# The ends of v's and z's tiles issued in steps behind the next tiles' products, and the up product's output in four DRAM buffers

## The chip, the cores and the metric

The kernel runs on one core of one Trainium2 chip. The metric is the device time of one execution in microseconds (us). Before the change the median of three runs is 2250.19 us (2246.54 to 2250.68). The engines of the core work beside each other, each through its own list of instructions in order: TensorE (PE) does the matrix products, VectorE (DVE), ScalarE (ACT) and GpSimd (POOL) the elementwise work, and SyncE (SP) issues most of the transfers.

## The reference

One layer of a hybrid encoder: a gated MLP branch with a spatial mixer (u, v), a state-space branch (z, xBC, dt), gates, and a feed-forward part. 1024 prompt rows and 64 sample rows share the weights; the model width is 1024, everything is float32. Cut to what matters here:

```python
h = rms_norm(x, pre_mix_w)
u, v, z, xbc, dt_raw, g_a, g_b = jnp.split(h @ w_in, [p1, p2, p3, p4, p5, p6], axis=-1)
u = jax.nn.gelu(u)
v = layer_norm(jax.nn.gelu(v), gmlp_ln_w, gmlp_ln_b)
...
g = y * jax.nn.silu(z)          # gated group RMSNorm of the state-space branch
...
f = jnp.square(jax.nn.relu(rms_norm(x, pre_ffn_w) @ w_up)) @ w_down
x = x + rms_norm(f, post_ffn_w)
```

v has 1024 columns and z has 2048. The hidden width of the feed-forward part is 4096.

## The kernel before

**Stages.** The kernel goes through the first half of z's columns, then v together with z's second half, then the state-space stage, u with the spatial mixer, the two branch products, the output product, the up product and the down product. A float32 product is made of three matmuls on split operands: each operand is a high part (`split`, ACT, line 87) and a low part that is left over (line 88, DVE or POOL).

**z's first half** (lines 442 to 507). `z_tile` multiplies nine row tiles (eight of 128 prompt rows and the sample's) and ends each with a tanh on ACT (L453), a combine on DVE (L454) and a store from POOL's queue (L455).

**v and z's second half** (lines 506 to 582, called here the product stage). Each is a block of 1024 columns; v is `b = 0`, z's part `b = 1`. Rows and columns are halved, and a Strassen-like plan of seven products, `P2, P1, P6, P5, P7, P3, P4`, makes the four quarters. A product has four tiles of 128 rows by 512 columns (`m` = 0 to 3), each of 12 matmuls (lines 517 to 519), and the 64 sample rows go along in separate small products (`sample`). Chained products add into the four PSUM banks `X`: P1, P6, P7 and P4 go into the same bank of a tile one after the other, and the bank is read in between. P2, P5 and P3 use other banks, `ps`. What follows each tile:

- P2: ACT copies `ps` out (`cz`, L551). P6 and P5: ACT copies too (L557, L560), and after P5 DVE adds (L561).
- P1, P7, P3: DVE adds (L553, L563, L566), then the tile is finished with `epi`. P4's tiles are finished from PSUM directly.
- `epi` (lines 313 to 332) for v is a gelu with LayerNorm sums: square on ACT (L319), scale on POOL (L320), product on DVE (L321), tanh on ACT (L322), combine on DVE (L324), store from POOL's queue (L325), then three ACT instructions that form the sums (L330 to L332). For z it is a silu: tanh on ACT (L317), combine on DVE, store.
- `sample_out` (line 346) first folds the sample's two halves of partitions together with a transfer from SBUF to SBUF (`su`, L354) and an addition (L355), then calls `epi`.

After each tile, work for later products is slipped in: for even `m` a weight piece of the next product is split (`prep`), for odd `m` a piece of the product after that is loaded and, on POOL, added up (`build`, lines 389 to 404).

**Buffers.** The tiles `cz`, `c1`, `c5`, `sbs`, `sc` and `su` share eight buffers (tag `s2`), the working tiles `t` and `jk` of `epi` three (tag `tm`).

**Order.** The program is written once, and a scheduler that keeps a timeline decides in which order each engine gets its instructions; the engines then work through them in that order. An instruction whose input isn't there holds up what is behind it on its engine.

**Up and down products.** `up` writes its output in the combinations that the down product's seven products read (`C` and `E`, lines 1311 to 1316) into the DRAM tensors `rc_d` and `rs_d` (lines 1317 to 1321), 16 slices `p` one after the other. The down product takes four slices at a time (`b` = 0 to 3): `load_x` reads `rc_d` (L1373), `xs_load` reads `rs_d` (L1480), `load_w` the weights (L1379), and POOL sums weight pieces (L1384). `bcast` spreads `post_ffn_w` over the partitions (L191) for the last step.

Of the kernel before, what the change touches and what calls it, by code (L numbers as in the profile page):

```python
# [15 lines left out]
P = 128  # L16
# [17 lines left out]
TQ = 272  # L34
# [12 lines left out]
def program(tc, a):  # L47
# [3 lines left out]
    with ctx:  # L51
# [17 lines left out]
        rc_d = dram.tile([7, 16, P, 2, TQ], F32, name="rc_d")  # L69
        rs_d = dram.tile([16, P, 2, 64], F32, name="rs_d")  # L70
# [241 lines left out]

        def epi(pool, gelu, c, R, dst, inplace, st=None):

            t = pool.tile([P, 512], F32, tag="tm", bufs=tm_bufs[0], name="t")
            if not gelu:
                s.activation(t[:R], c[:R], AF.Tanh, scale=0.5)  # L317
            else:
                s.activation(t[:R], c[:R], AF.Square)  # L319
                g.tensor_scalar(out=t[:R], in0=t[:R], scalar1=GC * GA3, scalar2=GC, op0=ALU.mult, op1=ALU.add)  # L320
                v.tensor_tensor(out=t[:R], in0=c[:R], in1=t[:R], op=ALU.mult)  # L321
                s.activation(t[:R], t[:R], AF.Tanh)  # L322
            o = c if inplace else t
            v.scalar_tensor_tensor(out=o[:R], in0=t[:R], scalar=1.0, in1=c[:R], op0=ALU.add, op1=ALU.mult)  # L324
            g.dma_start(out=dst, in_=o[:R])  # L325
            if gelu:
                i, l = st
                jk = pool.tile([P, 512], F32, tag="tm", bufs=tm_bufs[0], name="jk")
                sm, nm = vsm[:R, l, i:i + 1], vnm[:R, l, i:i + 1]
                s.activation(jk[:R], o[:R], AF.Copy, accum_out=sm)  # L330
                s.activation(nm, sm, AF.Copy, scale=-1.0 / 512)
                s.activation(jk[:R], o[:R], AF.Square, bias=nm, accum_out=vm2[:R, l, i:i + 1])  # L332
# [14 lines left out]
        def sample_out(pool, gelu, ps, add, dst, st=None):  # L347

            c = pool.tile([P, 512], F32, tag="s2", bufs=s2_bufs[0], name="sc")
            u = pool.tile([P, 512], F32, tag="s2", bufs=s2_bufs[0], name="su")  # L350
            s.activation(c, ps, AF.Copy)
            if add is not None:
                v.tensor_tensor(out=c, in0=add, in1=c, op=ALU.add)
            nc.sync.dma_start(out=u[:64], in_=c[64:128, :])  # L354
            v.tensor_tensor(out=c[:64], in0=c[:64], in1=u[:64], op=ALU.add)  # L355
            epi(pool, gelu, c, 64, dst, True, st)
# [58 lines left out]
        with tc.tile_pool(name="p0", bufs=1, side="right") as p0:  # L415
# [26 lines left out]
            def z_tile(ws, gi, i):  # L442
                R = ROWS[i]
                dst = z_d[i * P:i * P + R, gi * 512:(gi + 1) * 512]
                if i == 8:
                    ps = mm.tile([P, 512], F32, tag="mm", name="ps")
                    sample(ps, 0, lambda q: ws[q], True, False)
                    sample(ps, 1, lambda q: ws[2 + q], False, True)
                    sample_out(p0, False, ps, None, dst)
                    return  # L450
# [36 lines left out]
            for i in range(NT):  # L487
                z_tile(ws, 0, i)
                first(i + 3)
                first_T(i + 2)  # L490
# [3 lines left out]
            for k, i in enumerate((4, 5, 6, 7, 8, 0, 1, 2, 3)):  # L494
                z_tile(ws, 1, i)
                if k in (0, 2, 4, 6):
                    sums_a(k // 2)
# [6 lines left out]
            prep(0, 1)  # L504

        with tc.tile_pool(name="pm", bufs=1, side="right") as pm, tc.tile_pool(name="xp1", bufs=3, space=PSUM) as xp:
            pmx.append(pm)
            s2_bufs[0], tm_bufs[0] = 8, 3
# [20 lines left out]
            for k, (b, n) in enumerate(plan):  # L529
# [12 lines left out]
                for m in range(4):  # L542
                    ps = X[m] if chained else mm.tile([P, 512], F32, tag="mm", name="ps")
                    mms(ps, XN[n], k, m, n == "P1" or not chained, chained)
                    if m % 2 == 0:
                        prep(k + 1, m // 2)
                    else:
                        build(k + 2, m // 2)
                    if n == "P2":
                        cz[m] = s2("cz")  # L550
                        s.activation(cz[m], ps, AF.Copy)  # L551
                    elif n == "P1":
                        v.tensor_tensor(out=cz[m], in0=ps, in1=cz[m], op=ALU.add)  # L553
                        epi(pm, gelu, cz[m], P, out_rows(b, m, 0), True, (m, 0))
# [7 lines left out]
                    elif n == "P7":  # L562
                        v.tensor_tensor(out=c5[m], in0=ps, in1=c5[m], op=ALU.add)  # L563
                        epi(pm, gelu, c5[m], P, out_rows(b, 4 + m, 1), True, (4 + m, 1))
                    elif n == "P3":
                        v.tensor_tensor(out=c1[m], in0=ps, in1=c1[m], op=ALU.add)  # L566
                        epi(pm, gelu, c1[m], P, out_rows(b, m, 1), True, (m, 1))
                    else:
                        epi(pm, gelu, ps, P, out_rows(b, 4 + m, 0), False, (4 + m, 0))
                if n == "P1":  # L570
                    sample(sa, 0, w, True, False)
                    sample_out(pm, gelu, sa, sbs, out_rows(b, 8, 0), (8, 0))
                elif n == "P5":
                    sample(sa, 0, w, False, False)
                elif n == "P3":
                    sample(sa, 1, w, False, True)
                    sample_out(pm, gelu, sa, None, out_rows(b, 8, 1), (8, 1))
                if n == "P1" and b == 1:
                    v_stats()
                if n == "P7" and b == 1:  # L580
                    for d, x in b12_parts():
                        nc.sync.dma_start(out=x, in_=d)
        ectx.close()
# [646 lines left out]
        def up_pass(p, tt, prev):  # L1230
# [83 lines left out]
            def post2():  # L1314
                v.tensor_tensor(out=E[:, 1], in0=C[:, 3], in1=E[:, 0], op=ALU.subtract)
                v.tensor_tensor(out=E[:, 3], in0=C[:, 1], in1=E[:, 1], op=ALU.subtract)
                nc.sync.dma_start(out=rc_d[0:2, p, :, tt].rearrange("o p c -> p o c"), in_=C[:, 0:2])
                nc.sync.dma_start(out=rc_d[2, p, :, tt], in_=C[:, 3])
                nc.sync.dma_start(out=rc_d[3:7, p, :, tt].rearrange("o p c -> p o c"), in_=E)
                for hh in range(2):  # L1320
                    nc.sync.dma_start(out=rs_d[p][:, :, hh * 32 + tt * 16:hh * 32 + tt * 16 + 16], in_=C[:, 2 * hh:2 * hh + 2, 256:TQ])
# [25 lines left out]
        bcast(pf, a["post_ffn_w"][0])  # L1347
# [17 lines left out]
        def xload(n, b):  # L1365
            res = []
            for q in range(2):
# [3 lines left out]
                src = rc_d[n, b * 4 + q * 2:b * 4 + q * 2 + 2]  # L1371
# [103 lines left out]
        def xs_load(b):  # L1475
# [3 lines left out]
            for j in range(2):  # L1479
                nc.sync.dma_start(out=raw[:, j], in_=rs_d[b * 4:b * 4 + 4][:, :, j, :].rearrange("q p c -> p q c"))  # L1480
# [15 lines left out]
        xsr = xs_load(0)  # L1496
        load_w(0, "w11")
        load_x(1)
# [4 lines left out]
        for k, (b, n) in enumerate(plan):  # L1503
            last = b == 3
            sl = slots[b]
            if n == "P2":
# [103 lines left out]
```

## Time and profile before

| | us |
|---|---|
| median of three runs | 2250.19 |
| the profiled execution | 2253.99 |
| its span | 2252.3 |
| TensorE busy | 2164.1 (96%) |
| VectorE busy | 1405.2 (62%) |
| ScalarE busy | 966.9 (43%) |
| GpSimd busy | 905.1 (40%) |

Times in the trace count from the start of the span. z's first half takes about the first 140 us, the product stage runs from there to about 310 us, the state-space stage follows; up runs from about 1540 to 1910 us, and down to the end. In the views a row names an engine, the tile written, an arrow and the tile read, and the line (L321 is line 321 of the kernel); a bracket with an arrow gives how long the engine had been idle before and what ended it. "PEclk" is the granted clock of TensorE as a share of full speed.

### The profile page before, as it was taken

What the parts mean: (1) busy time and instruction counts of PE and PEld (TensorE: products, weight loads), DVE (VectorE), ACT (ScalarE), POOL (GpSimd) and SP (SyncE); (2) the same over time, 40 slices, a digit from 0 to 9 for tenths busy, and PEclk for the clock granted to TensorE, in tenths of its full rate; (3) what the DMA queues carried; (4) which work ended last, traced back from release to release, by engine and by line L of the source; (5) the groups of instructions that cost most, each with busy time, mean ns of one, the idle gap of its engine ahead of it and who ended that gap; (6) DMA issues with size and microseconds to landing.
All of it is one profiled execution on the core that took longest, in us unless ns stands there. A gap on an engine that the chain in (4) does not pass through costs nothing.

```text
span 2252.3 us, 33407 instructions
## 1 busy us (share of the span) xinstructions
PE 2164.1 (96%) x12547; PEld 1951.4 (87%) x12547; DVE 1405.2 (62%) x1934; ACT 966.9 (43%) x1911; POOL 905.1 (40%) x888
## 2 busy tenths in 40 slices
PE   8998899999989999999999999998999998999997
PEld 6777689879979879889999999777999998888885
DVE  5846557677677767646632247377555556677777
ACT  5335636355445455433321123245555554433333
POOL 2644421472562652754512545353222223132134
PEclk9999899999999999999999999999999999999999
DMA  6255462253342351542353445443555447534543
GB/s 221 71 182 181 128 203 56 80 138 83 96 129 76 104 143 46 142 134 76 97 170 120 146 118 169 138 164 101 161 153 152 135 154 253 164 106 142 173 122 112
DMA packets 327994, 300.50 MB, mean 133 GB/s; under 512 B 40906, under 2 KB 286364, under 8 KB 327320
## 3 DMA queue, kind: packets, MB, share of 16 engines
q1 hardware_dynamic: 295720, 260.12, 38.8%
q10 hardware_dynamic: 27152, 22.29, 3.0%
q0 software_dynamic: 4960, 15.95, 2.0%
q8 instruction: 99, 1.62, 0.3%
q14 instruction: 63, 0.52, 0.1%
HBM read 220.49 MB, written 77.03 MB: 132 GB/s over the span
## 4 chain that ended last, share of the span: by engine, by line
PE 72%; DVE 7%; DMA 6%; POOL 6%; issue 5%; ACT 3%; SPq 0%; ACTq 0%; POOLq 0%; DVEq 0%
PE ps L125 8%; PE ps L127 8%; PE ps L126 8%; PE X L1241 3%; PE X L1240 3%; PE X L1242 3%; PE X L1391 2%; PE X L1392 2%; PE X L1390 2%; PE ps L978 2%; PE ps L979 2%; PE ps L980 2%; PE ps L1390 2%; DMA bc<-ac_d 2%; PE ps L1392 2%
## 5 line engine op out<-in xcount | busy, mean ns | idle before, releaser
L127 PE MATMUL ps<-hTh,wl 128*128 128x384 f32 (+1 forms) x1152 | 386.5, 336 | 0.0
L125 PE MATMUL ps<-hTh,wh 128*128 128x384 f32 (+1 forms) x1152 | 384.2, 334 | 0.0
L126 PE MATMUL ps<-hTl,wh 128*128 128x384 f32 (+1 forms) x1152 | 384.1, 333 | 0.0
L88 POOL TENSOR_TENSOR wl<-raw,wh 128x1024 fp32r<-128x1024 f32 x74 | 181.8, 2458 | 251.4 <-ACT wh L87 251.4
L127 PEld LDWEIGHTS ps<-hTh,wl 128*128 128x128 f32 x1152 | 217.0, 188 | 9.6 <-issue 9.1
L126 PEld LDWEIGHTS ps<-hTl,wh 128*128 128x128 f32 x1152 | 217.2, 189 | 7.2 <-issue 7.1
L125 PEld LDWEIGHTS ps<-hTh,wh 128*128 128x128 f32 x1152 | 217.1, 188 | 6.6 <-issue 5.6
L87 ACT ACTIVATE wh<-raw 128x1024 fp32r<-128x1024 f32 (+1 forms) x113 | 118.6, 1051 | 239.9 <-PE ps L126 92.7
L643 DVE SCALAR_TENSOR_TENSOR acc<-raw,cw,acc 128x384 f32<-128x384 f32 (+1 forms) x216 | 135.4, 627 | 31.5 <-ACT acc L641 25.4
L1240 PE MATMUL X<-hb,wu 128*128 128x272 f32 x512 | 147.5, 290 | 1.3 <-ACT ev L1247 1.0
L1241 PE MATMUL X<-hb,wu 128*128 128x272 f32 x512 | 147.9, 290 | 0.0
L1242 PE MATMUL X<-hb,wu 128*128 128x272 f32 x512 | 146.1, 290 | 0.0
L1384 POOL TENSOR_TENSOR wd<-wd,wd 128x1024 f32<-128x1024 f32 x32 | 86.0, 2690 | 112.3 <-DVE dl L88 73.2
L762 ACT ACTIVATE bc<-bc,pcum 128x128 f32<-128x128 f32 (+1 forms) x288 | 90.4, 384 | 83.0 <-POOL bc L759 82.8
L979 PE MATMUL ps<-ob,wh 128*128 128x384 f32 (+1 forms) x384 | 125.4, 327 | 0.0
L978 PE MATMUL ps<-ob,wh 128*128 128x384 f32 (+1 forms) x384 | 125.4, 326 | 0.0
L980 PE MATMUL ps<-ob,wl 128*128 128x384 f32 (+1 forms) x384 | 125.3, 326 | 0.0
L87 ACT ACTIVATE dh<-wd 128x1024 fp32r<-128x1024 f32 x56 | 59.0, 1054 | 148.9 <-PE ps L1391 89.8
L88 DVE TENSOR_TENSOR dl<-wd,dh 128x1024 fp32r<-128x1024 f32 x56 | 71.3, 1278 | 47.5 <-ACT dh L87 45.7
L1391 PE MATMUL X<-dl,dh 128*128 128x512 f32 x256 | 99.2, 390 | 0.0
L1392 PE MATMUL X<-dh,dl 128*128 128x512 f32 x256 | 98.9, 389 | 0.0
L88 DVE TENSOR_TENSOR dl<-xd,dh 128x1024 fp32r<-128x1024 f32 x56 | 98.0, 1775 | 1.5 <-PE X L1242 1.2
(459 smaller groups left out, 6022.2 us busy)
## 6 DMA issues: line engine op xcount, KB each, us to landing
raw<-w_in SPq DMA_DIRECT2D x56, 512.0 KB, 4.0
xd<-rc_d SPq DMA_DIRECT2D x112, 256.0 KB, 4.0
rc_d<-E SPq DMA_DIRECT2D x32, 544.0 KB, 3.0
bc<-ac_d SPq DMA_DIRECT2D x64, 256.0 KB, 4.3
raw<-w_branch_b SPq DMA_DIRECT2D x32, 512.0 KB, 3.8
wr<-w_up SPq DMA_DIRECT2D x32, 512.0 KB, 4.0
wd<-w_down SPq DMA_DIRECT2D x16, 1024.0 KB, 5.7
w<-w_in SPq DMA_DIRECT2D x28, 512.0 KB, 3.7
```

Of the source, the lines that this page charges most:

```text
L87: s.activation(hi, src, AF.Copy)
L88: (lo_eng or v).tensor_tensor(out=lo, in0=src, in1=hi, op=ALU.subtract)
L125: pe.matmul(ps[:, :n], wh[:, k, :], hh[:, k, :n], start=(k == 0), stop=False)
L126: pe.matmul(ps[:, :n], wh[:, k, :], hl[:, k, :n], start=False, stop=False)
L127: pe.matmul(ps[:, :n], wl[:, k, :], hh[:, k, :n], start=False, stop=(k == 7))
L978: pe.matmul(ps[:, :n], wh[:, k, :], ob[:, kk, :], start=(k == 0), stop=False)
L979: pe.matmul(ps[:, :n], wh[:, k, :], ob[:, 4 + kk, :], start=False, stop=False)
L980: pe.matmul(ps[:, :n], wl[:, k, :], ob[:, kk, :], start=False, stop=(k == 7))
L1240: pe.matmul(ps, wh[:, k, :], bh[:, k, :], start=start and k == 0, stop=False, skip_group_check=chain)
L1241: pe.matmul(ps, wh[:, k, :], bl[:, k, :], start=False, stop=False, skip_group_check=chain)
L1242: pe.matmul(ps, wl[:, k, :], bh[:, k, :], start=False, stop=k == 3, skip_group_check=chain)
L1392: pe.matmul(ps, xl, wh, start=False, stop=q == 3, skip_group_check=chain)
```

## The change

`epi` and `sample_out` become generators. `end(x)` runs the first step of a tile's end at once and keeps the rest in the list `ends`; `advance(old)` runs one more step of every end that was in the list before the present tile. A gelu end has three steps: square and scale; product and tanh; combine, store and sums. A silu end has two, and the sample's end has one more ahead, up to the `su` transfer. After each tile of the product stage the older ends move one step on, after the new tile's own eviction; at the end of a stage the list is emptied. In z's halves ahead of it only the sample's end is taken in steps. The `tm` tag gets a fourth buffer, and where the result is written in place the sums reuse `t` for their unused output.

`rc_d` and `rs_d` become four tensors each, one for each group of four slices. In the down product the second operand load is written ahead of one weight load, and the broadcast of `post_ffn_w` is written at the third group in place of the beginning.

```diff
-        rc_d = dram.tile([7, 16, P, 2, TQ], F32, name="rc_d")
-        rs_d = dram.tile([16, P, 2, 64], F32, name="rs_d")
+        rc_d = [dram.tile([7, 4, P, 2, TQ], F32, name=f"rc{b}_d") for b in range(4)]
+        rs_d = [dram.tile([4, P, 2, 64], F32, name=f"rs{b}_d") for b in range(4)]
...
+        ends = []
+
+        def end(x):
+            next(x, None)
+            ends.append(x)
+
+        def advance(xs):
+            for x in xs:
+                if next(x, True):
+                    ends.remove(x)
+
         def epi(pool, gelu, c, R, dst, inplace, st=None):
...
                 s.activation(t[:R], c[:R], AF.Square)
                 g.tensor_scalar(out=t[:R], in0=t[:R], scalar1=GC * GA3, scalar2=GC, op0=ALU.mult, op1=ALU.add)
+                yield
                 v.tensor_tensor(out=t[:R], in0=c[:R], in1=t[:R], op=ALU.mult)
                 s.activation(t[:R], t[:R], AF.Tanh)
+            yield
             o = c if inplace else t
...
-                jk = pool.tile([P, 512], F32, tag="tm", bufs=tm_bufs[0], name="jk")
+                jk = t if inplace else pool.tile([P, 512], F32, tag="tm", bufs=tm_bufs[0], name="jk")
...
             nc.sync.dma_start(out=u[:64], in_=c[64:128, :])
+            yield
             v.tensor_tensor(out=c[:64], in0=c[:64], in1=u[:64], op=ALU.add)
-            epi(pool, gelu, c, 64, dst, True, st)
+            yield from epi(pool, gelu, c, 64, dst, True, st)
...
-            s2_bufs[0], tm_bufs[0] = 8, 3
+            s2_bufs[0], tm_bufs[0] = 8, 4
...
+                    old = list(ends)
                     if n == "P2":
                         cz[m] = s2("cz")
                         s.activation(cz[m], ps, AF.Copy)
                     elif n == "P1":
                         v.tensor_tensor(out=cz[m], in0=ps, in1=cz[m], op=ALU.add)
-                        epi(pm, gelu, cz[m], P, out_rows(b, m, 0), True, (m, 0))
+                        end(epi(pm, gelu, cz[m], P, out_rows(b, m, 0), True, (m, 0)))
...
+                    advance(old)
...
+            while ends:
+                advance(list(ends))
...
-        bcast(pf, a["post_ffn_w"][0])
...
-                src = rc_d[n, b * 4 + q * 2:b * 4 + q * 2 + 2]
+                src = rc_d[b][n, q * 2:q * 2 + 2]
...
         xsr = xs_load(0)
+        load_x(1)
         load_w(0, "w11")
-        load_x(1)
...
+            if b == 2 and n == "P2":
+                bcast(pf, a["post_ffn_w"][0])
```

**What moves.** ACT at the turn from v to z, before the change. L551 is z's first eviction, L319 with `X` the square of a tile of v's P4, L330 and L332 the sums of tiles of v's P3 (`c`):

```order
L319 ACTIVATE t<-c_1311 128x512
L331 ACTIVATE vnm<-vsm 128x1
L551 ACTIVATE cz<-ps 128x512
L332 ACTIVATE jk,vm_95<-c_1292,vnm 128x512
L87 ACTIVATE wh<-v_1790 128x1024
L551 ACTIVATE cz<-ps 128x512
L87 ACTIVATE wh<-v_1832 128x1024
L322 ACTIVATE t<-t 128x512
L330 ACTIVATE jk,vsm<-c_1311 128x512
L319 ACTIVATE t<-sc 64x512
```

The same place after the change (L332 is now the square, L336 the tanh, L345 to L347 the sums, L574 z's first eviction):

```order
L345 ACTIVATE t,vsm<-c_1312 128x512
L88 ACTIVATE wh<-w_1654 128x1024
L332 ACTIVATE t<-X 128x512
L346 ACTIVATE vnm<-vsm 128x1
L336 ACTIVATE t<-t 128x512
L88 ACTIVATE wh<-w_1712 128x1024
L347 ACTIVATE t,vm_101<-c_1312,vnm 128x512
L559 ACTIVATE sbs<-sb__1725 128x512
L336 ACTIVATE t<-t 64x512
L332 ACTIVATE t<-X 128x512
L574 ACTIVATE cz<-ps 128x512
```

The squares of two of v's P4 tiles, which stood behind z's evictions, now stand ahead of the first of them, and the sums of v's last P3 tile are done before it.

DVE at the same turn, after the change. L335 is the product, L339 the combine, L89 the low part of a weight piece (`w` for z's P2 and `v` for a later one), L576 the addition after z's P1; the combine that reads `X` is the last to read that bank:

```order
L335 TENSOR_TENSOR t<-X,t 128x512
L89 TENSOR_TENSOR wl<-w_1654,wh 128x1024
L339 SCALAR_TENSOR_TENSOR t<-t,X 128x512
L335 TENSOR_TENSOR t<-sc,t 64x512
L89 TENSOR_TENSOR wl<-w_1712,wh 128x1024
L339 SCALAR_TENSOR_TENSOR sc<-t,sc 64x512
L335 TENSOR_TENSOR t<-X,t 128x512 x2
L339 SCALAR_TENSOR_TENSOR t<-t,X 128x512 x2
L89 TENSOR_TENSOR wl<-v_1776,wh 128x1024
L576 TENSOR_TENSOR cz<-X,cz 128x512
```

Before the change every combine that read `X` stood behind the second weight piece `v` and the first addition of z's P1; now three stand ahead of that.

DVE near the first tiles of v's P5, after the change. L371 folds the sample's halves with `su`, L584 is the addition after P5:

```order
L371 TENSOR_TENSOR sc<-sc,su 64x512
L339 SCALAR_TENSOR_TENSOR cz<-t,cz 128x512
L335 TENSOR_TENSOR t<-sc,t 64x512
L89 TENSOR_TENSOR wl<-v_1258,wh 128x1024
L339 SCALAR_TENSOR_TENSOR sc<-t,sc 64x512
L584 TENSOR_TENSOR c_1233<-ps,c_1233 128x512
```

Before, the fold was followed by a product and a combine of one tile of P1 and by two such pieces, and then came the addition. Now a combine of P1, one piece and the sample's own product and combine stand between them.

On SP, around the last slices of up and the first loads of down, the rows after the change name other tensors and stand in the order they had before: `xd` from `rc_d` (L1398, L1373 before), the weights (L1404), and the broadcast (L192).

```order
L1344 DMA rc_d<-C 128x272
L1347 DMA rs_d<-C 256x1x16
L1343 DMA rc_d<-C 128x2x272
L1347 DMA rs_d<-C 256x1x16
L1345 DMA rc_d<-E 128x4x272
L1398 DMA xd<-rc_d 128x2x256 x2
L192 DMA fin_18236<-post_ffn_w 128x1024
L1441 DMA fin_18237<-x_d 128x1024 x2
```

More of the change, by code (lines that the diff above doesn't have):

```diff
@@ L448, in z_tile @@
                     sample(ps, 1, lambda q: ws[2 + q], False, True)
-                    sample_out(p0, False, ps, None, dst)
+                    end(sample_out(p0, False, ps, None, dst))
                     return
@@ L494, in program @@
             for k, i in enumerate((4, 5, 6, 7, 8, 0, 1, 2, 3)):
+                old = list(ends)
                 z_tile(ws, 1, i)
+                advance(old)
                 if k in (0, 2, 4, 6):
@@ L548, in program @@
                         build(k + 2, m // 2)
+                    old = list(ends)
                     if n == "P2":
@@ L563, in program @@
                         v.tensor_tensor(out=c5[m], in0=ps, in1=c5[m], op=ALU.add)
-                        epi(pm, gelu, c5[m], P, out_rows(b, 4 + m, 1), True, (4 + m, 1))
+                        end(epi(pm, gelu, c5[m], P, out_rows(b, 4 + m, 1), True, (4 + m, 1)))
                     elif n == "P3":
                         v.tensor_tensor(out=c1[m], in0=ps, in1=c1[m], op=ALU.add)
-                        epi(pm, gelu, c1[m], P, out_rows(b, m, 1), True, (m, 1))
+                        end(epi(pm, gelu, c1[m], P, out_rows(b, m, 1), True, (m, 1)))
                     else:
-                        epi(pm, gelu, ps, P, out_rows(b, 4 + m, 0), False, (4 + m, 0))
+                        end(epi(pm, gelu, ps, P, out_rows(b, 4 + m, 0), False, (4 + m, 0)))
+                    advance(old)
                 if n == "P1":
                     sample(sa, 0, w, True, False)
-                    sample_out(pm, gelu, sa, sbs, out_rows(b, 8, 0), (8, 0))
+                    end(sample_out(pm, gelu, sa, sbs, out_rows(b, 8, 0), (8, 0)))
                 elif n == "P5":
@@ L576, in program @@
                     sample(sa, 1, w, False, True)
-                    sample_out(pm, gelu, sa, None, out_rows(b, 8, 1), (8, 1))
+                    end(sample_out(pm, gelu, sa, None, out_rows(b, 8, 1), (8, 1)))
                 if n == "P1" and b == 1:
@@ L582, in program @@
                         nc.sync.dma_start(out=x, in_=d)
+            while ends:
+                advance(list(ends))
         ectx.close()
@@ L1479, in xs_load @@
             for j in range(2):
-                nc.sync.dma_start(out=raw[:, j], in_=rs_d[b * 4:b * 4 + 4][:, :, j, :].rearrange("q p c -> p q c"))
+                nc.sync.dma_start(out=raw[:, j], in_=rs_d[b][:, :, j, :].rearrange("q p c -> p q c"))
             return raw
```

8 lines of the change are left out of this document (4 added, 4 removed).

## The prediction

> **What bounds the kernel now.** I read the page first: TensorE (PE) is busy nearly all the time, so a change of the other engines is worth only what TensorE waits for them.
>
> ```profile
> span 2252.3 us, 33407 instructions
> PE 2164.1 (96%) x12547; PEld 1951.4 (87%) x12547; DVE 1405.2 (62%) x1934; ACT 966.9 (43%) x1911; POOL 905.1 (40%) x888
> ```
>
> 2252.3 - 2164.1 leaves 88 us of TensorE's idle time in the whole span, and the view of what TensorE waited for says where (us in total, times, longest):
>
> ```profile
> PE X L517 <- DVE t L324: 5.6, 1, 5.6
> PE X L1390 <- ACT dh L87: 4.1, 1, 4.1
> PE ps L517 <- ACT cz L551: 3.7, 1, 3.7
> PE ps L517 <- DVE c L561: 3.6, 1, 3.6
> PE s L1400 <- DVE xss L88: 3.1, 1, 3.1
> PE ps L139 <- DVE sz L454: 2.7, 1, 2.7
> PE X L517 <- DVE cz L553: 2.6, 1, 2.6
> PE ps L517 <- DVE c L566: 0.9, 1, 0.9
> ```
>
> Five rows have line 517, the first of each three product matmuls in the stage that the change rewrites: 5.6 + 3.7 + 3.6 + 2.6 + 0.9 = **16.4 us**. L139 is z's first half. L1390 and L1400 are the start of the down product.
>
> A stall costs more than its own length here. The windows view (columns: length, busy us of PE, PEld, DVE, ACT, POOL with counts, PEclk, DMA share, GB/s) over stretches that I cut where the granted clock changes:
>
> ```profile
> 96.75:103.57 6.82, 6.16 (x15) 4.81 (x16) 6.72 (x9) 2.95 (x5) 4.26 (x4) 0.50 0.10 40
> 171.84:175.25 3.41, 2.87 (x7) 2.29 (x8) 1.78 (x3) 1.33 (x3) 0.59 (x1) 0.50 0.83 317
> 226.45:233.28 6.83, 5.91 (x14) 4.67 (x15) 2.60 (x2) 4.86 (x13) 6.36 (x4) 0.50 0.55 176
> 243.52:250.35 6.83, 3.51 (x8) 2.81 (x9) 2.27 (x4) 4.73 (x12) 1.96 (x4) 0.50 0.19 58
> ```
>
> Matmuls start 0.43 us apart in such a stretch and 0.23 us apart at the full clock, as the timeline of TensorE shows around three of the stalls:
>
> ```profile
> 97.41 0.79 PE L139 MATMUL ps<-wh,hTh 128*128 128x512 f32 x1 [2.67 <-DVE sz L454]
> ...
> 227.37 0.80 PE L517 MATMUL ps<-wh,hTh 128*128 128x512 f32 x1 [3.66 <-ACT cz L551]
> ...
> 228.39 0.63 PE L519 MATMUL ps<-wh,hTl 128*128 128x512 f32 x1
> 228.82 0.63 PE L517 MATMUL ps<-wh,hTh 128*128 128x512 f32 x1
> ...
> 238.21 0.47 PE L517 MATMUL X<-wh,e4h 128*128 128x512 f32 x1 [2.57 <-DVE cz L553]
> ...
> 238.75 0.39 PE L519 MATMUL X<-wh,e4l 128*128 128x512 f32 x1
> 238.98 0.40 PE L517 MATMUL X<-wh,e4h 128*128 128x512 f32 x1
> ```
>
> So the stalls that end at 172.4, 227.4 and 246.8 us are followed by 7 + 14 + 8 matmuls at half speed, each 0.20 us too long: 1.4 + 2.8 + 1.6 = 5.8 us. The 2.67 us stall of z's first half, at 97.4, lies in such a stretch too; the 2.57 us at 238.2 brought none. What the stage loses is 16.4 + 5.8 = **22.2 us**, and no more than that can be won there.
>
> The Trainium skill's page "TensorE: Matmul & The Clock Gate" (Part 1) puts this drop to half clock behind at least one idle window of about 3.4 us. By that rule the 2.67 us stall should have cost nothing beside itself, and a first stall that shrinks from 3.6 to 3.2 (below) would save its 1.4 us more, for a sum of 2232.6. The trace differs at 97.4, so I let a stall near 3 us cost its half clock, which needs no threshold.
>
> **The change, part by part.** First, the ends. Each tile's end is a chain over three engines (for v: ACT square, POOL, DVE, ACT tanh, DVE, then ACT's sums), and the old program put a tile's whole chain ahead of the next tile's eviction. The worst place, in the timelines of ACT, DVE and POOL:
>
> ```profile
> 225.50 0.63 ACT L330 ACTIVATE jk<-c 128x512 f32<-128x512 f32 x1 [5.00 <-DVE c L324]
> ...
> 226.75 0.57 ACT L551 ACTIVATE cz<-ps 128x512 f32<-128x512 f32 x1
> ...
> 219.27 3.43 DVE L88 TENSOR_TENSOR wl<-w,wh 128x1024 fp32r<-128x1024 f32 x1
> 222.62 2.85 DVE L324 SCALAR_TENSOR_TENSOR c<-t,c 128x512 f32<-128x512 f32 x1
> ...
> 237.98 0.68 DVE L324 SCALAR_TENSOR_TENSOR c<-t,c 128x512 f32<-128x512 f32 x1
> ...
> 221.69 3.23 POOL L391 TENSOR_TENSOR v<-v,w 128x1024 f32<-128x1024 f32 x1
> ```
>
> z's first eviction (L551) needs only its product, but stands behind the sum of an old v tile (L330), which sat 5.00 us for L324. L324 itself took 2.85 us beside POOL's weight sums. In the new order v's last sum of that kind (now L345) stands ten rows ahead of z's first eviction (L574), with squares, a tanh and two splits between, so this 3.7 + 2.8 goes; if its combine is late all the same, the price is that of the second rival. What follows it in the queue moves too: each end issues a square, POOL's scale, a DVE product, a tanh, a DVE combine, a DMA from POOL's queue and three sums, the same number as before, one or two tiles later (12 matmuls of 0.23, 2.8 us, each). Their instructions are not cheaper or dearer, and reusing t for the sums only frees a buffer. On POOL the output DMA of a tile may now stand behind one more weight sum, up to 3.23 us; who waits for it is the tile that takes its s2 buffer, at least four tiles (11 us) later, so I cost that at nothing, and at 3.23 less what is left of the 11 if it isn't hidden.
>
> The largest stall, 5.6 us, has the same root. z's P1 writes into the banks X that v's P4 leaves, and their readers came late, one tile at a time:
>
> ```profile
> 243.41 0.57 ACT L319 ACTIVATE t<-X 128x512 f32<-128x512 f32 x1
> ...
> 245.44 0.63 ACT L322 ACTIVATE t<-t 128x512 f32<-128x512 f32 x1 [0.52 <-DVE t L321]
> ...
> 246.10 0.69 DVE L324 SCALAR_TENSOR_TENSOR t<-t,X 128x512 f32<-128x512 f32 x1 [0.69 <-ACT t L322]
> ...
> 250.15 0.69 DVE L324 SCALAR_TENSOR_TENSOR t<-t,X 128x512 f32<-128x512 f32 x1 [0.69 <-ACT t L322]
> ```
>
> The serial chain gives a tile every 250.15 - 246.10 = 4.05 us, against TensorE's 2.8. In steps the chains of two or three tiles overlap, and a tile costs what one engine has of it: on ACT 0.57 + 0.63 + 0.63 and a second sum like the first, about 2.5 with little left for short ones, near TensorE's pace. The new order has the squares of the first two X ahead of z's first eviction on ACT, and the last DVE reader of the first between z's two weight splits. So the stalls of 5.6 + 1.6, 2.6 (L553, behind the same splits and ends) and 0.9 (L566) go as well. Four of the five stalls together: 22.2 less the first, 3.6 + 1.4 = 5.0, leaves **17.2 us**.
>
> The first one I leave in. DVE and ACT there before:
>
> ```profile
> 162.08 2.40 DVE L355 TENSOR_TENSOR sc<-sc,su 64x512 f32<-64x512 f32 x1 [3.26 <-DMA su<-sc]
> ...
> 165.80 3.44 DVE L88 TENSOR_TENSOR wl<-v,wh 128x1024 fp32r<-128x1024 f32 x1
> ...
> 169.77 1.21 DVE L88 TENSOR_TENSOR wl<-v,wh 128x1024 fp32r<-128x1024 f32 x1
> 171.64 0.69 DVE L561 TENSOR_TENSOR c<-ps,c 128x512 f32<-128x512 f32 x1 [0.65 <-ACT c L560]
> ...
> 170.14 0.59 POOL L325 DMA_DIRECT2D v_d<-cz  x1 [1.98 <-DVE cz L324]
> ```
>
> TensorE waits for the L561 of 171.64. In the new order the sample's sum (now L371), a combine (L339), the sample's product (L335), a split (L89) and the sample's combine still stand ahead of it (now L584), and the sample's transfer starts no sooner. From 162.08: 2.40, a combine 0.69, a DMA issue of 0.59 and a scale of about as much on POOL, a product 0.69, the split 1.21 to 3.44, a combine 0.69. L584 then starts at 169.0 to 171.2, 2.6 to 0.4 us sooner than L561. With both combines at the 2.85 of 222.62 it is 2 x 2.16 later, up to 3.9 after L561. The stall is bounded by 1.0 and 7.5. POOL's weight sum runs beside the split, so I take the slow split; its 3.2 I leave at the old 3.6 with its 1.4, since 0.4 is within what the transfer's arrival (a wait of 3.26) can shift.
>
> Against the 17.2 stands one new thing: v's last ends now come while z's P2 and P1 run, and P1 writes the four X at four places, each after a DVE reader one or two tiles behind. From the order, with the durations above, three of these have 1 to 4 us to spare and the first about none. I put 1 us for it, between nothing and the 4.05 of one serial chain step. **Forecast saving: 17.2 - 1.0 = 16.2 us.**
>
> Second, z's first half. Apart from the sample's end, instructions stand in the same order and wait for the same; the 2.7 stays. Third, the DRAM buffers, the load that goes ahead of another and the later broadcast: on SP the loads of the down product stand in the same places as before, behind the same writes, and so on the other engines. The stall of L1390 stays (from the list of DMA issues and the timelines of DVE and POOL):
>
> ```profile
> xd<-rc_d SPq DMA_DIRECT2D x112, 256.0 KB, 4.0
> ...
> 1897.81 2.63 DVE L1311 TENSOR_TENSOR E<-C 128x272 f32<-128x272 f32 x1
> ...
> 1903.03 0.44 DVE L1315 TENSOR_TENSOR E<-C,E 128x272 f32<-128x272 f32 x1
> ...
> 1894.40 8.29 POOL L1384 TENSOR_TENSOR wd<-wd,wd 128x1024 f32<-128x1024 f32 x3
> ```
>
> DVE is slow here beside POOL's sums (2.63 against 0.44 us), not because of which DRAM buffer is read; the loads' own 4.0 us lie under the up product's last matmuls, before as after. I cost all this at 0, with 7.2 us (4.1 + 3.1) as the gain if it went, and 2 us either way for a few rows that are swapped at the start of the up product.
>
> **Sum.** The profiled execution took 2253.99 us (span 2252.3 and 1.7 around it) and would take 2237.8. The runs' median is 3.8 us below that execution, 2250.19; less 16.2 it gives **2234.0 us**.
>
> **The rivals.** *The first stall goes too*: the split runs at 1.21 us, L584 comes 2.6 us sooner, and the rest stays under what halves the clock. Then 5.0 more are saved less a rest of 1: 2230. For it: ACT evicts earlier; against it: the su transfer and POOL. *The stalls come back elsewhere*: DVE runs in order, so a combine that now stands ahead of an eviction may sit beside POOL's sums, 2.85 against 0.68 us, as at 222.62 and 237.98. Two such meetings of 2.2 us and one more stall with half clock (3.7 + 2.8) cost 10.9: 2244.9.
>
> The Trainium skill's page "SBUF — State Buffer" (section on the two separate sides) has VectorE operations with two SBUF inputs and GpSimd reads shut each other out for a whole instruction. By that rule, against this change, a meeting costs up to POOL's 3.23 us instead of 2.2, and this rival would come to 2247; that a combine grows from 0.68 to 2.85 beside POOL agrees with it.
>
> *The down product gains as well*: 2234.0 - 7.2 = 2227; against it, the same rows on SP. *Nothing happens*: the ends were no cause; 2250. *Slower*: one mechanism, the banks X. If every one of the four is released as late as the first was (5.6 and 1.6 of half clock), P1 of z loses 4 x 7.2 = 28.8 where it now loses 5.6 + 1.6 + 2.6 = 9.8. The other gains are 17.2 - 9.8 = 7.4, so the sum is 28.8 - 9.8 - 7.4 = 11.6 slower: 2262. It decides when the four waits with their half clock pass 17.2 us together, 4.3 each; against it, the squares of the first two X now stand ahead of z's evictions.
>
> **How the numbers follow.** Chances: forecast 0.52, first stall too 0.18, stalls come back 0.14, down too 0.04, nothing 0.06, slower 0.06. About 0.2% (4.5 us) is what a measurement of this kernel can tell from no change. Faster: 0.52 + 0.18 + 0.04 and two thirds of 0.14 (2245 lies near the edge), 0.83. Same: 0.06 and most of the rest of the 0.14, 0.10. Slower: 0.07. For the range, the forecast's own bounds (first stall 1.0 to 7.5, X 0 to 4, up 2 either way) give about 2227 to 2243; with the stalls that come back it reaches 2247, and with the first stall's rival and some of the down case 2224.
>
> **What would show it.** Right: no stall over 1 us at z's evictions and products, the clock at 1.00 from 190 to 300 us, the first stall near 172 us still there with its 3.4 us of half clock, and the same 4.1 and 3.1 at the down product's start. Wrong: a TensorE wait for X behind DVE's combine in z's P1, a weight split of 3.4 us ahead of an eviction, or new waits in up.

## The result

The changed kernel takes 2234.42 us (median of four runs, 2234.12 to 2235.93), the kernel before 2250.43 us beside it: a ratio of 0.9934, with a 95% interval of 0.9916 to 0.9951, or 16.0 us less. Run again later, in six runs beside three other kernels, it gave 2237.06 against 2251.42 us, 0.9939 (0.9925 to 0.9952).

The page and TensorE's waits after the change:

```profile
span 2232.7 us, 33419 instructions
PE 2157.4 (97%) x12547; PEld 1946.7 (87%) x12547; DVE 1407.1 (63%) x1934; ACT 964.7 (43%) x1911; POOL 908.6 (41%) x888
```

```profile
PE ps L539 <- DVE c L584: 5.6, 1, 5.6
...
PE X L1415 <- ACT dh L88: 4.1, 1, 4.1
...
PE s L1425 <- DVE xss L89: 2.8, 1, 2.8
PE ps L140 <- DVE sz L470: 2.7, 1, 2.7
```

Of the five stalls of the product stage one is left, the first, and it has grown from 3.6 to 5.6 us. The two at the start of the down product (4.1 and 2.8, before 4.1 and 3.1) and the one in z's first half (2.7) are where they were. The windows view (same columns as in the prediction):

```profile
97.58:100.99 3.41, 3.41 (x9) 2.65 (x10) 3.41 (x6) 2.18 (x4) 1.65 (x2) 0.50 0.21 79
169.25:176.08 6.83, 3.24 (x8) 2.59 (x9) 6.12 (x6) 4.43 (x11) 2.98 (x2) 0.50 0.69 187
190.00:300.00 110.00, 110.00 (x482) 88.11 (x481) 76.16 (x87) 66.65 (x136) 59.20 (x62) 1.00 0.64 197
1889.57:1896.40 6.83, 4.06 (x10) 2.27 (x9) 5.23 (x6) 1.47 (x2) 3.89 (x3) 0.50 0.37 113
```

From 190 to 300 us TensorE is busy for all 110.00 us at the full clock. The first stall still has half clock behind it, 8 matmuls, 1.6 us. How much the stage gained is best read from the first and the last start of one form of its matmuls, the ones that write the banks X from `hTh`, here of the kernel before and then of the changed one. (The stage's very first matmul, of v's P2, starts earlier still: at 123.3 us before, not at the 140 us given further up.)

```profile
L517 PE MATMUL X<-wh,hTh x96: 387/389/793, 135.1 to 314.8; 128*128 128x512 f32 x96
```

```profile
L539 PE MATMUL X<-wh,hTh x96: 387/389/397, 134.0 to 297.3; 128*128 128x512 f32 x96
```

314.8 - 135.1 = 179.7 us before, 297.3 - 134.0 = 163.3 us after: 16.4 us, about as much as the whole median moved. This length, called "the stage" below, is free of the scatter that other parts of the kernel add to a single execution; between the two profiles of the changed kernel (here and run 9) it differs by 0.8 us.

At the turn from v to z, ACT now runs the squares of v's P4 tiles early (L332 with `X`; L574 is z's eviction):

```profile
213.90 0.57 ACT L332 ACTIVATE t<-X 128x512 f32<-128x512 f32 x1
...
218.32 0.58 ACT L332 ACTIVATE t<-X 128x512 f32<-128x512 f32 x1
218.79 0.58 ACT L574 ACTIVATE cz<-ps 128x512 f32<-128x512 f32 x1
...
226.49 0.60 ACT L332 ACTIVATE t<-X 128x512 f32<-128x512 f32 x1
```

Before the change the four squares ran from 243.41 to 255.56 us. Now the first is at 209.54, three stand ahead of z's first eviction, the four are spread over 17 us, and TensorE waits for none of the four banks.

### The profile page after: what moved, and what is told of

The parts are those of the page before. It is cut to its first block, busy times and chain, and to the rows that moved or that the text cites. A ratio compares the mean times of both kernels' runs of the same rounds, so it can differ in the third digit from the quotient of the medians.

```text
span 2232.7 us, 33419 instructions
## 1 busy us (share of the span) xinstructions
PE 2157.4 (97%) x12547; PEld 1946.7 (87%) x12547; DVE 1407.1 (63%) x1934; ACT 964.7 (43%) x1911; POOL 908.6 (41%) x888
## 4 chain that ended last, share of the span: by engine, by line
PE 74%; POOL 7%; DVE 6%; DMA 5%; issue 5%; ACT 2%; SPq 0%; ACTq 0%; POOLq 0%; DVEq 0%
PE ps L126 8%; PE ps L128 8%; PE ps L127 8%; PE X L1267 3%; PE X L1266 3%; PE X L1268 3%; PE X L1416 2%; PE X L1417 2%; PE X L1415 2%; PE ps L1005 2%; PE ps L1004 2%; PE ps L1006 2%; PE ps L1415 2%; PE ps L1417 2%; PE ps L1416 2%
## 5 line engine op out<-in xcount | busy, mean ns | idle before, releaser
L89 POOL TENSOR_TENSOR wl<-raw,wh 128x1024 fp32r<-128x1024 f32 x74 | 181.2, 2450 | 251.6 <-ACT wh L88 251.6
L89 DVE TENSOR_TENSOR dl<-wd,dh 128x1024 fp32r<-128x1024 f32 x56 | 71.4, 1281 | 47.6 <-ACT dh L88 45.7
L1416 PE MATMUL X<-dl,dh 128*128 128x512 f32 x256 | 99.2, 390 | 0.0
L89 DVE TENSOR_TENSOR dl<-xd,dh 128x1024 fp32r<-128x1024 f32 x56 | 98.0, 1775 | 1.5 <-PE X L1268 1.2
```

The costliest lines, as they stand in the source:

```text
L89: (lo_eng or v).tensor_tensor(out=lo, in0=src, in1=hi, op=ALU.subtract)
L1416: pe.matmul(ps, xh, wl, start=False, stop=False, skip_group_check=chain)
```

## The experiments

All are compared with the kernel before on the same chip; the ratio is of the medians with its 95% interval, the stage is from the one profile of each kernel.

| run | us | before | ratio | stage us |
|---|---|---|---|---|
| before (first profile) | | 2250.43 | | 179.7 |
| changed kernel | 2234.42 | 2250.43 | 0.9934 (0.9916 to 0.9951) | 163.3 |
| 1 DRAM part only | 2251.31 | 2250.24 | 1.0001 (0.999 to 1.0012) | 180.6 |
| 2 working buffers, no steps | 2235.32 | 2250.24 | 0.993 (0.9915 to 0.9946) | 164.9 |
| 3 fourth buffer only | 2252.17 | 2250.24 | 1.001 (1.0 to 1.0019) | 180.2 |
| 4 steps, jk of its own | 2237.70 | 2250.24 | 0.994 (0.9921 to 0.9959) | 166.1 |
| 5 reuse, three buffers | 2239.40 | 2249.56 | 0.9955 (0.9938 to 0.9972) | 168.8 |
| 6 jk in its own ring | 2235.99 | 2249.56 | 0.9943 (0.9924 to 0.9961) | 165.0 |
| 7 su from ACT's queue | 2236.55 | 2249.56 | 0.994 (0.9921 to 0.9958) | 163.7 |
| 8 no POOL sum for P7 | 2231.07 | 2249.56 | 0.9917 (0.9899 to 0.9935) | 160.5 |
| 9 changed kernel again | 2237.06 | 2251.42 | 0.9939 (0.9925 to 0.9952) | 164.1 |
| 10 P7's sum on DVE | 2233.89 | 2251.42 | 0.9922 (0.9908 to 0.9937) | 162.6 |
| 11 down sums on DVE | 2239.26 | 2251.42 | 0.9948 (0.9934 to 0.9962) | 163.9 |
| 12 both on DVE | 2233.88 | 2251.42 | 0.9927 (0.9909 to 0.9945) | 160.8 |

### 1. The DRAM part alone

```diff
 (the kernel before, with)
+        rc_d = [dram.tile([7, 4, P, 2, TQ], F32, name=f"rc{b}_d") for b in range(4)]
+        rs_d = [dram.tile([4, P, 2, 64], F32, name=f"rs{b}_d") for b in range(4)]
...
-        bcast(pf, a["post_ffn_w"][0])
...
+        load_x(1)
         load_w(0, "w11")
-        load_x(1)
...
+            if b == 2 and n == "P2":
+                bcast(pf, a["post_ffn_w"][0])
```

> The kernel before with only the second part of the change: rc_d and rs_d in four tensors, the second operand load ahead of a weight load, the broadcast at the third group. Theory (the ends in the product stage carry the whole gain; this part is worth 0): within 4 us of the kernel before, about 2250 us, the five product-stage stalls (16.4 us) and the two at the start of the down product (4.1 and 3.1 us) all still there. Rival (the smaller buffers let the first down loads start earlier): about 2241 us, the 4.1 and 3.1 us stalls and the half clock after them gone.

No change: 1.0001. TensorE's waits of that kernel have both stalls of the down product:

```profile
PE X L1389 <- ACT dh L87: 4.1, 1, 4.1
PE X L517 <- DVE t L324: 4.1, 1, 4.1
...
PE s L1399 <- DVE xss L88: 3.0, 1, 3.0
```

On the kernel before, the quarter buffers, the load order and the later broadcast together are worth nothing that can be told from noise, and the rival that gave the down product a gain is out.

### 2 to 4. Steps or buffers

The prediction put the gain down to the steps and costed the buffers at nothing. Three kernels take the two apart.

```diff
 2 (the kernel before, with)
-            s2_bufs[0], tm_bufs[0] = 8, 3
+            s2_bufs[0], tm_bufs[0] = 8, 4
-                jk = pool.tile([P, 512], F32, tag="tm", bufs=tm_bufs[0], name="jk")
+                jk = t if inplace else pool.tile([P, 512], F32, tag="tm", bufs=tm_bufs[0], name="jk")
```

> The kernel before with only the working buffers of the change: four tm buffers, and t reused for the sums' unused output; no generators, no steps, every end still written in one go behind its own tile. Theory S (the steps carry the gain, as the prediction put it, buffers only make room): the stalls of 5.6, 3.7 and 2.6 us stay for the most part, 2244 to 2250 us. Theory B (each v end held two of three tm buffers, so that ends could only run one after the other; freeing them is what lets the ends overlap): the stalls after 190 us go, about 2234 to 2238 us.

```diff
 3 (the kernel before, with)
-            s2_bufs[0], tm_bufs[0] = 8, 3
+            s2_bufs[0], tm_bufs[0] = 8, 4
```

> The kernel before with only a fourth tm buffer, t and jk still two tiles. Theory S: as before, 2250 us. Theory B, if the number of buffers decides: two ends fit at once instead of one and a half, at least the 5.6 us stall shrinks, 2240 to 2246 us; if it is the reuse of t that decides, 2250 us.

```diff
 4 (the changed kernel, with)
-                jk = t if inplace else pool.tile([P, 512], F32, tag="tm", bufs=tm_bufs[0], name="jk")
+                jk = pool.tile([P, 512], F32, tag="tm", bufs=tm_bufs[0], name="jk")
```

> The changed kernel, but the sums write their unused output into a tile jk of their own again; steps and four tm buffers stay. Theory S (steps): 2234 to 2237 us, no stall over 1 us between 190 and 300 us. Theory B (reuse of t): at least one of the later stalls is back, 2240 to 2250 us.

Without any step the buffers give 14.9 us (2), and without the reuse the steps, beside the fourth buffer, give 12.5 us (4); their intervals and that of the changed kernel overlap for the most part. The fourth buffer alone gives nothing (3). Steps with three buffers were not run. ACT's timelines show what the working buffers do. The squares of v's P4 tiles, in the kernel with only the fourth buffer:

```profile
242.09 0.57 ACT L319 ACTIVATE t<-X 128x512 f32<-128x512 f32 x1
...
246.14 0.58 ACT L319 ACTIVATE t<-X 128x512 f32<-128x512 f32 x1
```

They start at 242 us, 4.05 us apart, as in the kernel before. With the reuse and no steps:

```profile
210.58 0.57 ACT L319 ACTIVATE t<-X 128x512 f32<-128x512 f32 x1
...
223.18 0.58 ACT L319 ACTIVATE t<-X 128x512 f32<-128x512 f32 x1
```

They start at 210.58, more than 30 us sooner, and what is left of the four later stalls is 0.76 us; one of 0.36 us, at z's P5, is new. In the kernel with steps and a jk of its own the X bank is waited for a little:

```profile
234.11 0.50 PE L539 MATMUL X<-wh,hTh 128*128 128x512 f32 x1 [1.11 <-DVE t L339]
```

So theory S is wrong as it was put, and so is B if it claims that only the reuse works: the reuse with a fourth buffer does nearly all of it, and so do the steps with a fourth buffer.

### 5 and 6. How many ends are open

In the kernel before, an end takes two buffers of the ring in turn, first t and then jk. With three buffers the second end after it can only take its t when the first end is done with one of them, so that about one and a half ends can be open at a time. Two more kernels ask whether the count of ends that can hold a t decides.

```diff
 5 (the kernel before, with)
-                jk = pool.tile([P, 512], F32, tag="tm", bufs=tm_bufs[0], name="jk")
+                jk = t if inplace else pool.tile([P, 512], F32, tag="tm", bufs=tm_bufs[0], name="jk")
```

> The kernel before with only the reuse of t for the sums' unused output; three tm buffers as before, no steps. Theory B2 (what matters is how many ends can be open at once: with t and jk in one ring of three, one and a half; with reuse three): the stalls of 5.6, 3.7 and 2.6 us go, 2234 to 2239 us. Rival (it takes reuse and the fourth buffer together): 2243 us or more, one of these stalls left.

```diff
 6 (the kernel before, with)
-                jk = pool.tile([P, 512], F32, tag="tm", bufs=tm_bufs[0], name="jk")
+                jk = pool.tile([P, 512], F32, tag="jk", bufs=1, name="jk")
```

> The kernel before with jk in a ring of its own with one buffer, beside the three tm buffers for t: four buffers in all, as many as in the run with only a fourth buffer, no reuse, no steps. Theory B2 (open ends): three t at once as with the reuse, so the same time as that run to within 3 us, 2234 to 2239 us. Rival (the reuse itself matters, since a sum that writes t needs no buffer at all): 2246 to 2250 us.

Run 6 has as many buffers in all as run 3, and jk is still written; only the ring is another. It gains 13.6 us where run 3 gains none, and ACT's squares show why:

```profile
212.03 0.60 ACT L319 ACTIVATE t<-X 128x512 f32<-128x512 f32 x1
...
214.57 0.58 ACT L319 ACTIVATE t<-X 128x512 f32<-128x512 f32 x1
```

These first two are 2.5 us apart and 30 us ahead of those of run 3. The runs in order of the ends that can hold a t at once, in place ends counted: one and a half (before) 179.7 us of stage, two (run 3) 180.2, three (runs 5 and 6) 168.8 and 165.0, four (run 2) 164.9. That fits a tile every 2.8 us whose end, one behind the other, takes 4.05 us: two are too few, three enough. I call it a reading that fits, since no run varied the count alone: in runs 5 and 2 the reuse comes with it.

The count holds for the ends that are written in place. P4's ends are not, so in runs 2 and 5 they still take t and jk from the ring, and in run 5 the last two squares of X are 4.07 us apart, much as before the change:

```profile
235.38 0.58 ACT L319 ACTIVATE t<-X 128x512 f32<-128x512 f32 x1
...
239.45 0.58 ACT L319 ACTIVATE t<-X 128x512 f32<-128x512 f32 x1
```

They come 16 us sooner all the same, since the ends ahead of them are no longer late. The first two squares of v's P7, which is written in place, in the kernel before:

```profile
184.56 0.63 ACT L319 ACTIVATE t<-c 128x512 f32<-128x512 f32 x1 [1.36 <-DVE c L563]
...
192.62 0.62 ACT L319 ACTIVATE t<-c 128x512 f32<-128x512 f32 x1
```

and in run 5:

```profile
183.67 0.63 ACT L319 ACTIVATE t<-c 128x512 f32<-128x512 f32 x1 [1.94 <-DVE c L563]
...
186.39 0.63 ACT L319 ACTIVATE t<-c 128x512 f32<-128x512 f32 x1 [2.09 <-DVE c L563]
```

With the reuse they are 2.7 us apart, the pace of the tiles, and each waits for its own sum on DVE (L563); before, they are 8.1 us apart. So the stalls at the turn to z look for the most part like a delay that had piled up over P7's and P3's ends, and not like the pace of P4's own; no run changed P4's ends alone.

Run 5 is the slowest of the four that gain (2, 4, 5 and 6). Its first stall is 6.4 us, and it has one more at z's eviction:

```profile
227.15 0.50 PE L517 MATMUL ps<-wh,hTh 128*128 128x512 f32 x1 [1.86 <-ACT cz L551]
```

### 7 and 8. What makes the first stall

The changed kernel's DVE before that stall:

```profile
162.99 2.46 DVE L371 TENSOR_TENSOR sc<-sc,su 64x512 f32<-64x512 f32 x1 [2.91 <-DMA su<-sc]
165.37 0.67 DVE L339 SCALAR_TENSOR_TENSOR cz<-t,cz 128x512 f32<-128x512 f32 x1
167.62 0.68 DVE L335 TENSOR_TENSOR t<-sc,t 64x512 f32<-64x512 f32 x1 [1.58 <-POOL t L333]
168.23 1.21 DVE L89 TENSOR_TENSOR wl<-v,wh 128x1024 fp32r<-128x1024 f32 x1
169.36 2.82 DVE L339 SCALAR_TENSOR_TENSOR sc<-t,sc 64x512 f32<-64x512 f32 x1
172.11 0.67 DVE L584 TENSOR_TENSOR c<-ps,c 128x512 f32<-128x512 f32 x1
```

and its POOL:

```profile
162.49 2.40 POOL L415 TENSOR_TENSOR v<-v,w 128x1024 f32<-128x1024 f32 x1 [3.27 <-issue]
...
167.67 3.98 POOL L415 TENSOR_TENSOR v<-v,w 128x1024 f32<-128x1024 f32 x1
```

This is the chain that the prediction wrote down, with the su transfer, the fold, the sample's product, one split and the sample's combine ahead of L584. Two of its rows are slow: the fold and the sample's combine each lie beside one of POOL's two weight sums.

```diff
 7 (the changed kernel, with)
-            nc.sync.dma_start(out=u[:64], in_=c[64:128, :])
+            s.dma_start(out=u[:64], in_=c[64:128, :])
```

> The changed kernel with the su transfer of the sample's fold issued from ACT's queue instead of SP's. Theory T (the first stall, 5.6 us, hangs on su, which lands 5.2 us after its issue behind a weight load on the same queue): su lands 2 to 3 us sooner and the stall shrinks by as much, about 2231 us. Theory P (POOL's weight sums beside DVE's fold and combine, 2.45 and 2.83 us there, set it): the stall stays over 4 us, 2233 to 2235 us.

```diff
 8 (the changed kernel, with)
                 t = w_piece(b, 1, 1, q, "v3", True)
-                u = w_piece(b, 0, 1, q, "w12", False)
-                tt_(out=t, in0=t, in1=u, op=ALU.add)
+                if b == 1:
+                    u = w_piece(b, 0, 1, q, "w12", False)
+                    tt_(out=t, in0=t, in1=u, op=ALU.add)
```

> The changed kernel without the load and the POOL sum of w12 in v's product P7 (so P7 of v is computed from w22 alone; everything else is kept). Theory P (POOL's sums beside DVE): the fold and the combine run at about 1.0 and 0.7 us instead of 2.45 and 2.83, the stall shrinks from 5.6 to 2 us or less and its half clock (1.7 us) may go, 2228 to 2231 us. Theory T (su's arrival): the stall stays over 4 us, 2233 to 2235 us.

Run 7: su's reader starts at 162.17 instead of 162.99 us, and the fold is as slow as before. The stall is 5.0 us:

```profile
162.17 2.67 DVE L371 TENSOR_TENSOR sc<-sc,su 64x512 f32<-64x512 f32 x1 [2.13 <-DMA su<-sc]
```

The time is not told from that of the changed kernel. The other queue is worth 0.8 us of arrival in this profile, not 2 to 3. Run 8 leaves w12 out of v's P7, so its v is not complete and only its time counts. DVE of that kernel, its TensorE wait, and a window that holds the stall:

```profile
163.49 0.68 DVE L371 TENSOR_TENSOR sc<-sc,su 64x512 f32<-64x512 f32 x1 [3.47 <-DMA su<-sc]
...
169.22 0.68 DVE L339 SCALAR_TENSOR_TENSOR sc<-t,sc 64x512 f32<-64x512 f32 x1
169.82 0.68 DVE L585 TENSOR_TENSOR c<-ps,c 128x512 f32<-128x512 f32 x1
```

```profile
PE ps L540 <- DVE c L585: 2.4, 1, 2.4
```

```profile
160.00:200.00 40.00, 37.58 (x163) 29.80 (x163) 26.16 (x35) 28.51 (x63) 16.35 (x17) 1.00 0.55 172
```

su is no sooner (163.49), but fold and combine run at 0.68 each, the stall is 2.4 us, and the clock stays at 1.00 through it. The 3.9 us that the two instructions lose beside POOL (2.46 and 2.82 against 0.68) and the 1.6 us of half clock are 5.5; the stall and its half clock shrank by 5.6 - 2.4 + 1.6 = 4.8. (The stage is only 2.8 to 3.6 us shorter, since z's first eviction now makes TensorE wait 1.2 us.) Theory P holds. On the way to L585 DVE still waits 3.47 us for su and 1.56 for POOL's scale and makes two splits (2.35); no run took apart what the 2.4 us that are left come from. The Trainium skill's page "SBUF — State Buffer" (section on the two separate sides) says that a VectorE operation with two SBUF inputs and a GpSimd operation that reads SBUF shut each other out for a whole instruction; the 0.68 that became 2.46 and 2.82 beside POOL's sums, and POOL's own 2.40 that became 3.98, agree with it.

### 9 to 12. Moving POOL's sums

```diff
 10 (the changed kernel, with)
-                tt_(out=t, in0=t, in1=u, op=ALU.add)
+                (v if b == 0 else g).tensor_tensor(out=t, in0=t, in1=u, op=ALU.add)
 11 (the changed kernel, with)
-        def wsum(dst, x, y, op_):
+        def wsum(dst, x, y, op_, eng=g):
...
-                g.tensor_tensor(out=wsl[dst][:, c, :], in0=wsl[x][:, c, :], in1=wsl[y][:, c, :], op=op_)
+                eng.tensor_tensor(out=wsl[dst][:, c, :], in0=wsl[x][:, c, :], in1=wsl[y][:, c, :], op=op_)
...
-                wsum(sl["v1"], sl["w11"], sl["w12"], ALU.subtract)
+                wsum(sl["v1"], sl["w11"], sl["w12"], ALU.subtract, v if b == 0 else g)
-                wsum(sl["v2"], sl["w22"], sl["v1"], ALU.subtract)
+                wsum(sl["v2"], sl["w22"], sl["v1"], ALU.subtract, v if b == 0 else g)
 12 (both)
```

> The changed kernel once more, beside the three that follow: 2233 to 2236 us, the first stall 5 to 6 us with its half clock, 4.1 and 2.8 us at the start of the down product.

> The changed kernel with the weight sum of v's P7 (the two pieces that POOL added while the sample's fold ran) on DVE. Theory P (POOL beside DVE sets the first stall): 2 x 1.2 us more work for DVE, but fold and combine at 0.7 each instead of 2.45 and 2.83, the stall at 2.5 to 4 us, 2230 to 2233 us. Rival (DVE in order now waits for the weight load and passes that on): the stall stays at 5 us or more, 2234 to 2236 us.

> The changed kernel with POOL's first four weight sums of the down product (v1 and v2 of its first quarter) on DVE. Theory P for the down product (the 4.1 us stall comes from DVE's E subtractions running at 2.63 instead of 0.44 us beside POOL's sums): both subtractions at about 0.5 us, the transfer of E issued 3 to 4 us sooner, the stalls of 4.1 and 2.8 us and the half clock (1.8 us) down to 3 us in all, 2228 to 2231 us. Rival (DVE has no room for 4 x 1.2 us there, or the loads land too late in any case): 2233 us or more.

> Both of these moves together on the changed kernel: if each is right, their gains add up, 2225 to 2230 us; if neither, 2234 us or more.

Run 9 came out about a microsecond above what was expected. In run 10, which keeps the loads that run 8 left out, both slow rows are gone too, two weight sums of 1.2 us stand ahead instead, and the stall is 3.4 us with 3.4 us of half clock:

```profile
163.49 1.22 DVE L415 TENSOR_TENSOR v<-v,w 128x1024 f32<-128x1024 f32 x1 [3.52 <-issue]
164.63 0.68 DVE L371 TENSOR_TENSOR sc<-sc,su 64x512 f32<-64x512 f32 x1
...
170.44 0.68 DVE L339 SCALAR_TENSOR_TENSOR sc<-t,sc 64x512 f32<-64x512 f32 x1
```

The stage is only 1.5 us shorter than in run 9, since z's first eviction now makes TensorE wait 1.2 us. By the medians run 10 is 3.2 us under the changed kernel, but the intervals overlap (0.9908 to 0.9937, 0.9925 to 0.9952): that it beats it isn't settled.

Run 11 was expected to shorten the down product's stalls and did not. DVE and POOL of that kernel:

```profile
1882.39 2.64 DVE L1337 TENSOR_TENSOR E<-C 128x272 f32<-128x272 f32 x1
1884.95 0.43 DVE L1338 TENSOR_TENSOR E<-C 128x272 f32<-128x272 f32 x1
```

```profile
1878.77 5.96 POOL L1409 TENSOR_TENSOR wd<-wd,wd 128x1024 f32<-128x1024 f32 x2 [40.59 <-DMA wd<-w_down]
```

POOL's next two sums took the place of those that went to DVE, so the first E subtraction still lies beside one, and one of the sums on DVE (at 1892.32) now stands ahead of the split of `xss` that TensorE waits for. The stalls there are 4.0 and 2.4 us, with 1.6 us more at L1416. The median is 2.2 us above run 9, with intervals that overlap. That POOL slows the E subtractions is seen again (2.64 against 0.43); that taking this away would end the stall isn't shown, since this run did not take it away. Run 12, both together, gives the median of run 10, above the 2225 to 2230 us that were expected if both gains were real; its stage is 160.8, and its down product waits 4.9, 2.0 and 1.8 us.

## Why the prediction was right, and where it wasn't

**The size.** Forecast 2234.0 us, a saving of 16.2; measured 2234.42 and 16.0, with the stage 16.4 us shorter. The term of 17.2 us, the four later stalls with their half clock, came out as forecast: all four are gone from 190 us on.

**The cause.** The forecast was right in its number and wrong in what brings it about. The step that failed is the sentence that steps move the old ends behind the new evictions while "reusing t for the sums only frees a buffer", a buffer costed at nothing. Run 2 gets the same time with the buffers and no step, run 4 nearly the same with the steps and without the reuse. What held the ends one behind the other was that each needed two buffers of a ring of three: with the program written in the old order, the scheduler moves them apart by itself as soon as three can be open (runs 2, 5 and 6). The steps do it in another way. A likely one, which no run shows, is that an end asks for jk only at its last step, so that the next ends' t come first. The stalls were read rightly as late ends; that "the old program put a tile's whole chain ahead of the next tile's eviction" was read as a matter of how the program is written, when it was what the ring allowed the scheduler. In the profile before this wait is not to be seen as such, since the squares simply stand late in ACT's order, and I never asked which instruction could first use which buffer.

**The first stall.** Kept at 3.6 with 1.4 of half clock, between bounds of 1.0 and 7.5; it is 5.6 with 1.6. The chain was the right one. Its slow end was put at the split, which ran at 1.21, and the combines at 0.69; instead the sample's combine took 2.82 beside POOL, the case that only the upper bound held. The mis-sized term is 2.2 us.

**The banks X.** 1.0 us was set aside for z's P1; the profile after shows no wait for X, and that of run 9 one of 0.7 for the sample's bank `sa`. This and the first stall pull opposite ways, 1.0 more saved and 2.2 less, so the terms would give 15.0, and the stage gained 16.4. The other 1.4 is in how the prediction priced a stall. Read from start to start, against the usual 0.23 us, the 3.66 us stall takes 223.33 to 227.37, so it loses 3.8, and the next matmul starts 0.59 us later and not 0.43. Summed so over the stage's matmuls from 123 us on, the kernel before loses 23.88 us, where 22.2 were reckoned, and the changed one 7.44, where the same reckoning gives 5.6 + 1.6 = 7.2: 16.44 between them. That the sum came out within 0.4 us is thus luck in part: 1.0 and 1.4 too little, 2.2 too much.

**The rivals.** "The first stall goes too" was wrong in the kernel and right about the way: without POOL's sums it comes to 2.4 us without half clock (run 8). "The stalls come back elsewhere" was right about the mechanism, a combine of 2.82 beside POOL, and it met just one place. The DRAM part is worth nothing, as costed (run 1). Slower by the banks X did not come.

**The rule on the clock.** The first stall was kept on the side where half clock follows, and 1.6 us of it did. The Trainium skill's page "TensorE: Matmul & The Clock Gate" (Part 1) asks for at least one idle window of about 3.4 us before the drop. This stall of 5.6 us agrees with it; the 2.7 us of z's first half, with half clock from 97.58 in the same profile, does not. What decides is taken up in the last section.

## What to carry to other kernels

Where an in-order engine shows one tile's chain after the other, look at how many buffers each chain takes from which ring before changing the order: a scratch tile that shares a ring with the chain's own working tile can halve the number of chains that can be open, and one more buffer in the shared ring need not help. When a change does two things that could each explain its gain, run each alone; here the reuse or the steps, each beside the fourth buffer, did nearly all of it, and the time agreed with a wrong reason. Elementwise work on two SBUF operands that is close to TensorE's path should not stand beside GpSimd's long sums (here 0.68 us became 2.5 to 2.8), and moving one sum away only helps if no other sum takes its place.

## What the runs showed of the hardware

The length of a stall doesn't decide by itself whether the clock is halved. Before the change 2.67 us was followed by half clock and 2.57 not; in run 8 2.42 not. In run 5 the 1.86 us stall at 227.15 was, from 227.86 on:

```profile
227.86:231.27 3.41, 3.41 (x10) 2.62 (x9) 0.69 (x1) 3.41 (x9) 3.17 (x3) 0.50 0.69 231
```

With the Trainium skill's page "TensorE: Matmul & The Clock Gate" (Part 1), one idle window of about 3.4 us, this does not agree: 1.86 us was enough.

All these stretches are 3.41 us long or a multiple of it, and their starts lie on a grid of that step: 96.75, 171.84, 226.45 and 243.52 in the kernel before are 22, 16 and 5 times 3.413 us apart. The runs place stalls differently against it. The grid window that holds most of the stall, for the stalls of 2.67 and 2.57 us before the change, then for run 5's 1.86 and run 8's 2.42:

```profile
93.34:96.75 3.41, 1.40 (x6) 0.67 (x5) 3.41 (x4) 0.00 (x0) 2.27 (x2) 1.00 0.01 1
236.69:240.11 3.42, 1.90 (x8) 1.61 (x9) 1.97 (x3) 1.69 (x6) 0.66 (x2) 1.00 0.19 77
224.45:227.86 3.41, 1.55 (x7) 1.00 (x6) 2.01 (x2) 1.97 (x8) 2.51 (x4) 1.00 1.02 395
168.97:172.38 3.41, 1.82 (x8) 1.52 (x9) 2.22 (x4) 3.08 (x9) 0.59 (x1) 1.00 0.90 263
```

TensorE is idle in them for 2.01, 1.52, 1.86 and 1.59 us, and the window behind the first and the third has half clock, the one behind the others not. The 2.57 us stall left its other 1.05 us, and that of run 8 0.83, to the window ahead; run 5's shorter one fell into a single window. All 14 profiles cut in this way, from 60 to 2200 us, agree. Each of the 77 windows at full clock with more than 1.9 us idle is followed by half clock, and no window with less than 1.4 us is; in between both occur. So in these runs it is idle time in one window of the grid, about half of it, that goes with the drop, and not the length of the stall. No run held a stall fixed and moved the grid.
